# FFN-up GEMM as 2x2x2 block products by Strassen's identity, with weight-block sums made by accumulating DMAs

## The chip, the cores and the metric

One core of one Trainium2 chip. The metric is device microseconds (us) of one execution. Engines are named as in the profile: PE is TensorE (matmuls; PEld its weight loads), DVE is VectorE, ACT is ScalarE, POOL is GpSimd, SP is SyncE, which here only issues DMAs.

## The reference

One step of a streaming encoder with two layers for 640 tokens (512 of a prompt, 8 x 16 of running streams), width 1024, in fp32. Each layer projects x, runs four attention and convolution branches, mixes them, and ends in an FFN. Only the FFN is touched (`d_ff` = 2816):

```python
x = layer_norm(ALPHA * x + mixed, ln1_g, ln1_b)
up = x @ w_up                                   # (640, 1024) @ (1024, 5632)
upc, new_ffn = causal_dwconv(up, past_ffn, ffn_conv_w, ffn_conv_b)   # 3 taps
val, gate = jnp.split(upc, 2, axis=-1)
h = (jax.nn.silu(gate) * val) @ w_down          # (640, 2816) @ (2816, 1024)
x = layer_norm(ALPHA * x + h, ln2_g, ln2_b)
```

## The kernel before

Activations lie transposed, channels on partitions and tokens along the columns. To keep fp32 accuracy every GEMM splits both operands into a high and a low part and does three matmuls for one (`mm3`, L113 to L116). `xh` and `xl` are the parts of x^T, 8 blocks of 128 channels by 640 tokens, in two chunks of tokens, `CH` = 384 + 256, since a PSUM buffer holds 512 columns. `wload` (L103 to L111) fetches 512 KB of weights by a DMA of SP into `wst` (2 buffers), ACT casts the high part `wh` (L108), DVE subtracts to the low part `wl` (L110); `wh` and `wl` are rings of 3. `mtile` (L118) makes 128 output channels from one such weight tile: for each chunk 8 blocks x 3 matmuls into a PSUM buffer `g` (3 buffers).

The FFN's 44 column tiles of w_up make 22 j's: tile j holds values, tile 22 + j gates. `up(j)` (L1093) calls `mtile` for both, copies the results to `ext` on ACT (L1101 to L1103), saves the last columns on POOL (`nf`, L1104, L1105), runs the 3-tap conv (L1108 on ACT, two steps of L1110 on DVE for each tile, into `uac`), then tanh on ACT (`eth`, L1114), three products on DVE (L1115, L1117, L1120), and the split of the result into `hh` (ACT, L1123) and `hl` (DVE, L1124), with 10 buffers each. I call what follows the last matmul of a j its tail.

The down GEMM (`rows_gemm`, L1035) takes the j's in parts, two j's to a pair: parts of 6, 6, 6 and 4 j's. A part runs after the up tiles of its j's, in two halves of 512 output columns; in a half each j gives 5 token tiles x 3 matmuls of 512 columns into PSUM buffers `a` (5) and one `g`, and DVE adds the sums to x (`acx`, L1043, L1045). The last two parts run at the end of the FFN. So PE works through phases of up tiles with down parts between them. The order on each engine is fixed at build time by a scheduler from the program's order and priorities; `wload` has a high priority, so that weights are asked for early.

Of the kernel before, what the change touches and what calls it, by code (L numbers as in the profile page):

```python
# [16 lines left out]
L = 2  # L17
D = 1024
# [16 lines left out]
CH = ((0, 384), (384, 640))  # L35
# [5 lines left out]
def body(tc, I, O):  # L41
# [28 lines left out]

    xh = [perm.tile([128, 8, b - a], F32R, name=f"xh{i}") for i, (a, b) in enumerate(CH)]
    xl = [perm.tile([128, 8, b - a], F32R, name=f"xl{i}") for i, (a, b) in enumerate(CH)]
# [40 lines left out]
    def mm3(ps, ah, al, bh, bl, first, last):  # L113
        pe.matmul(ps, lhsT=ah, rhs=bh, start=first, stop=False)  # L114
        pe.matmul(ps, lhsT=ah, rhs=bl, start=False, stop=False)  # L115
        pe.matmul(ps, lhsT=al, rhs=bh, start=False, stop=last)  # L116

    def mtile(src):  # L118
        wh, wl = wload(src)
        out = []  # L120
        for c, (a, b) in enumerate(CH):
            ps = gps()[:, : b - a]
            for k in range(8):
                mm3(ps, wh[:, k * 128 : k * 128 + 128], wl[:, k * 128 : k * 128 + 128],
                    xh[c][:, k, :], xl[c][:, k, :], k == 0, k == 7)
            out.append(ps)
        return out

    def mtiles(srcs):
        ws = [wload(s) for s in srcs]  # L130
        out = [[] for _ in srcs]
        for c, (a, b) in enumerate(CH):
            for i, (wh, wl) in enumerate(ws):
                ps = gps()[:, : b - a]
                for k in range(8):
                    mm3(ps, wh[:, k * 128 : k * 128 + 128], wl[:, k * 128 : k * 128 + 128],
                        xh[c][:, k, :], xl[c][:, k, :], k == 0, k == 7)
                out[i].append(ps)
        return out

    def xcol(t):
        return (0, t * 128) if t < 3 else (1, (t - 3) * 128)
# [23 lines left out]
    def x_transpose(z, t):  # L166
        c, o = xcol(t)
        for h in range(2):
# [4 lines left out]
            hi = xh[c][:, h * 4 : h * 4 + 4, o : o + 128]  # L173
            act.copy(hi, pv)  # L174
            dve.tensor_sub(xl[c][:, h * 4 : h * 4 + 4, o : o + 128], pv, hi.bitcast(F32))
# [78 lines left out]
def layer(tc, l, I, O, E):  # L254
# [59 lines left out]
    for k in range(2):  # L314
# [107 lines left out]
    for ps, (a, b) in zip(mtile(I["wa"][l, 0]), CH):  # L422
        act.copy(qih[:, a:b], ps)
        dve.tensor_sub(qil[:, a:b], ps, qih[:, a:b].bitcast(F32))
        if b == T:
            act.copy(qs, ps[:, 128:256])
    exts = []
    for k in range(2):
# [156 lines left out]
    for t in range(NT):  # L585
        c, o = xcol(t)
        g1 = gps()[:, :256]
        for k in range(8):
            wh, wl = w1[k // 4]
            ko = (k % 4) * 256  # L590
            mm3(g1, xh[c][:, k, o : o + 128], xl[c][:, k, o : o + 128],
# [422 lines left out]
    df, close_df = op("df", "right")  # L1014
    mh, ml = [], []
    for m in range(8):
# [3 lines left out]
        h_ = mk(df, "hh", T, 10, F32R)  # L1020
        l_ = mk(df, "hl", T, 10, F32R)
# [11 lines left out]
    ep, close_ep = op("ep")  # L1033

    def rows_gemm(parts, hh, hl, src, after):  # L1035
        for pi, kps in enumerate(parts):
# [15 lines left out]
            if not lastp:  # L1052
                for hf in range(2):
                    pst = [aps() if t < 4 else gps() for t in range(NT)]
# [7 lines left out]
            else:  # L1062
                ws = [[wload(src(kp, hf), p=ep, nb=4) for kp in kps] for hf in range(2)]
# [13 lines left out]
    gb = mk(dx, "gb", 2 * D).rearrange("p (i d) -> p i d", i=2)  # L1077
    sp.dma_start(gb, I["ln1"][l].partition_broadcast(128))

    after1 = (lambda t: ln_rows(dx, x[t], t, gb, [], t in (1, 3)), lambda t: x_transpose(x[t], t))  # L1080

    for _ in rows_gemm([[0, 1], [2, 3]], mh, ml, lambda kp, hf: I["wo"][l, hf, kp], after1):
        pass

    sf = mk(ep, "sf", 44 * 16)
# [3 lines left out]
    nfv = nf.rearrange("p (j i) -> p j i", j=44)  # L1089
    hh, hl = {}, {}  # L1090
    first = mtiles([I["wu"][l, jj] for jj in (0, NJ, 1)])

    def up(j):  # L1093
        accs = []
        for i_, jj in enumerate((j, NJ + j)):
# [238 lines left out]
```

## Time and profile before

| | |
|---|---|
| time, median of 3 runs | 2145.78 us (2144.29 to 2147.37) |
| profiled execution: span | 2143.2 us |
| median less this span | 2.6 us |
| PE busy | 2111.0 us, 13284 matmul records |
| DVE, ACT, POOL busy | 1368.2, 767.7, 366.3 us |
| mean granted TensorE clock | 0.997 of full speed |

The span runs from the first to the last instruction of one profiled execution; the durations below come from that execution. Shares are averages over stages with different limits; the FFN of layer 0 lies at about 620 to 1060 us, that of layer 1 at about 1675 to 2143 us.

### The profile page before, as it was taken

To read this page: it belongs to the slowest core of one execution; us is meant where nothing else is said; L and a number is where in the kernel's file an instruction comes from. 1 tells how busy PE (TensorE), PEld (TensorE's weight loads), DVE (VectorE), ACT (ScalarE), POOL (GpSimd) and SP (SyncE) were. 2 spreads that over 40 slices of the span, in tenths; PEclk is the share of its full clock that TensorE was granted. 3 is DMA by queue.
4 is the path that set the end of the run, shared out by engine and by line. 5 is a ranking of instruction groups with operands and counts; after the bars stand their busy time and mean duration, and the time that the engine had idled before them with its cause. 6 is when DMAs were issued, how large, how long until landed. Compare 5 with 4: busy or idle time off the path is not lost.

```text
span 2143.2 us, 33850 instructions
## 1 busy us (share of the span) xinstructions
PE 2111.0 (98%) x13284; PEld 1914.2 (89%) x13284; DVE 1368.2 (64%) x2399; ACT 767.7 (36%) x1520; POOL 366.3 (17%) x595
## 2 busy tenths in 40 slices
PE   6999999999999999999999999999999999999998
PEld 6998979879889898999899898897898998989996
DVE  5899994643476455555679999745246653645656
ACT  4333432322235243344224434223232442424440
POOL 2300001411022021122012000023021220202211
PEclk9999999999999999999999999999999999999999
DMA  8452124442422222222343521354314122222221
GB/s 262 113 167 83 64 87 130 154 135 89 149 75 80 78 70 79 79 70 89 116 113 91 172 80 52 119 156 141 108 62 172 70 71 78 79 70 79 80 85 70
DMA packets 110871, 220.52 MB, mean 103 GB/s; under 512 B 31148, under 2 KB 51408, under 8 KB 110192
## 3 DMA queue, kind: packets, MB, share of 16 engines
q1 hardware_dynamic: 110712, 218.36, 30.8%
q8 instruction: 104, 1.70, 0.3%
q14 instruction: 55, 0.45, 0.1%
HBM read 196.81 MB, written 21.50 MB: 102 GB/s over the span
## 4 chain that ended last, share of the span: by engine, by line
PE 93%; issue 2%; DVE 2%; POOL 2%; ACT 1%; DMA 1%; SPq 0%; POOLq 0%; DVEq 0%; ACTq 0%
PE g L114 22%; PE g L116 22%; PE g L115 21%; PE a L116 6%; PE a L114 6%; PE a L115 6%; PE a L725 1%; PE a L677 1%; PE a L913 1%; PE a L712 1%; PE a L949 1%; PE a L517 1%; PE a L171 1%; PE a L982 1%; PE a L766 0%
## 5 line engine op out<-in xcount | busy, mean ns | idle before, releaser
L114 PE MATMUL g<-xh,wh 128*128 128x256 f32 (+1 forms) x2784 | 867.0, 312 | 2.6 <-ACT xh L174 1.5
L115 PE MATMUL g<-xl,wh 128*128 128x256 f32 (+1 forms) x2784 | 866.0, 311 | 0.1
L116 PE MATMUL g<-xh,wl 128*128 128x256 f32 (+1 forms) x2784 | 863.6, 310 | 0.0
L114 PEld LDWEIGHTS g<-xh,wh 128*128 128x128 f32 x2784 | 524.2, 188 | 17.3 <-issue 9.4
L115 PEld LDWEIGHTS g<-xl,wh 128*128 128x128 f32 x2784 | 525.6, 189 | 6.7 <-issue 5.0
L116 PEld LDWEIGHTS g<-xh,wl 128*128 128x128 f32 x2784 | 525.1, 189 | 6.7 <-issue 5.8
L110 DVE TENSOR_TENSOR wl<-wst,wh 128x1024 fp32r<-128x1024 f32 (+1 forms) x248 | 302.0, 1219 | 338.1 <-ACT wh L108 337.8
L108 ACT CAST wh<-wst 128x1024 fp32r<-128x1024 f32 (+1 forms) x248 | 258.3, 1043 | 527.3 <-PE g L115 269.6
L116 PE MATMUL a<-wh,hl 128*128 128x512 f32 x512 | 202.6, 397 | 0.0
L115 PE MATMUL a<-wl,hh 128*128 128x512 f32 x512 | 201.5, 394 | 0.0
L114 PE MATMUL a<-wh,hh 128*128 128x512 f32 x512 | 200.9, 395 | 0.0
L1104 POOL COPY nf<-ext 128x2 f32<-128x2 f32 x88 | 93.4, 1061 | 478.6 <-ACT ext L1102 478.6
L1110 DVE SCALAR_TENSOR_TENSOR uac<-ext,pc,uac 128x656 f32<-128x656 f32 x176 | 158.3, 900 | 9.6 <-ACT uac L1108 0.4
L851 POOL TENSOR_TENSOR acx<-acx,gt 128x640 f32<-128x640 f32 x32 | 52.7, 1648 | 387.1 <-DVE gt L842 241.4
L115 PEld LDWEIGHTS a<-wl,hh 128*128 128x128 f32 x512 | 96.1, 188 | 23.5
L116 PEld LDWEIGHTS a<-wh,hl 128*128 128x128 f32 x512 | 96.1, 188 | 22.9
L114 PEld LDWEIGHTS a<-wh,hh 128*128 128x128 f32 x512 | 96.0, 188 | 22.2
L842 DVE SCALAR_TENSOR_TENSOR gt<-gt,g 128x384 f32<-128x384 f32 (+1 forms) x96 | 45.8, 483 | 106.0 <-PE g L116 106.0
L1101 ACT COPY ext<-g 128x384 f32<-128x384 f32 x88 | 42.2, 480 | 155.1 <-PE g L116 91.9
L826 ACT ACTIVATE gt<-g 128x384 f32<-128x384 f32 (+1 forms) x128 | 55.4, 433 | 112.9 <-PE g L116 109.2
L619 DVE SCALAR_TENSOR_TENSOR cacc<-cep,pc,cacc 128x512 f32<-128x512 f32 x120 | 89.6, 747 | 0.1
L1108 ACT ACTIVATE uac<-ext,pc 128x656 f32<-128x656 f32 x88 | 82.8, 941 | 4.7 <-ACT ext L1103 0.4
(316 smaller groups left out, 2831.6 us busy)
## 6 DMA issues: line engine op xcount, KB each, us to landing
wst<-in_wu SPq DMA_DIRECT2D x88, 512.0 KB, 3.5
wst<-in_wg SPq DMA_DIRECT2D x64, 512.0 KB, 3.8
wst<-in_wd SPq DMA_DIRECT2D x44, 512.0 KB, 3.6
wst<-in_wa SPq DMA_DIRECT2D x22, 512.0 KB, 3.5
wbs<-in_wb SPq DMA_DIRECT2D x64, 128.0 KB, 2.2
cd<-in_c_bv SPq DMA_DIRECT2D x32, 256.0 KB, 3.9
ca<-in_c_bkT SPq DMA_DIRECT2D x32, 256.0 KB, 2.7
wst<-in_wo SPq DMA_DIRECT2D x16, 512.0 KB, 3.5
```

The source lines that it names most:

```text
L108: act.copy(wh[:, :cols], st[:, :cols])
L110: dve.tensor_sub(wl[:, :cols], st[:, :cols], wh[:, :cols].bitcast(F32))
L114: pe.matmul(ps, lhsT=ah, rhs=bh, start=first, stop=False)
L115: pe.matmul(ps, lhsT=ah, rhs=bl, start=False, stop=False)
L116: pe.matmul(ps, lhsT=al, rhs=bh, start=False, stop=last)
L619: dve.scalar_tensor_tensor(a_[:, 0:TP], ep_[:, j : j + TP], w, a_[:, 0:TP], op0=ALU.mult, op1=ALU.add)
L826: act.activation(g_[:, a:b], ps, AF.Tanh, scale=0.5)
L842: dve.scalar_tensor_tensor(dst[:, a:b], g_[:, a:b], 1.0, ps, op0=ALU.add, op1=ALU.mult)
L851: pool.tensor_tensor(acc[m], acc[m], g_, op=ALU.add)
L1104: pool.tensor_copy(nfv[:, jj, 0:2], ext[:, 512:514])
L1108: act.activation(ac, ext[:, 2:658], AF.Identity, scale=wc[2], bias=pc[:, PC_FB + jj : PC_FB + jj + 1])
L1110: dve.scalar_tensor_tensor(ac, ext[:, i : i + 656], wc[i], ac, op0=ALU.mult, op1=ALU.add)
```

## The change

Chunks become 320 + 320 tokens (`HT` = 320), and `xh` and `xl` one tile each. For j = 0 and 1 the up tiles are made as before. For j = 2 to 21 the value and the gate tile are taken together: w_up's block for j is [k-half 0, k-half 1] x [gates, values], x^T is [k-half 0, k-half 1] x [tokens 0 to 319, 320 to 639], and the 2 x 2 result comes from seven products instead of eight (`seven`), each of 4 blocks x 3 matmuls of 320 columns. The sums of x blocks, T1 to T4, are made once a layer on DVE from a raw copy of x^T (`raw`, written by ACT at the transposes) and split to parts (`split_t`). The sums of weight blocks are made for each j in a staging tile `sg` of 7 blocks (2 buffers): SP's DMAs fill it with 1.79 MB, and three DMAs issued by POOL add to it in place; four casts and four subtractions turn it into `wh` and `wl`, in the same ring of 3 as the down weights.

Three PSUM buffers collect the products: A takes a11, s2, s3, a22 one after the other, C takes s1 and s4, B takes a12; between them ACT copies A to `sn` tiles, and DVE and ACT form the four blocks in `ext` from these. The conv and the rest of `up` are unchanged. `ext` has 3 buffers instead of 2, `hh` and `hl` 6 instead of 10; the down parts are 2, 4, 4, 4, 4 and 4 j's, the first four of them each after its own j's, the last two at the end, so that the up phases have 2 + 4, 4, 4 and 8 j's. Down parts use `a` alone.

```diff
-CH = ((0, 384), (384, 640))
+HT = 320
+CH = ((0, HT), (HT, 640))
...
-    def x_transpose(z, t):
+    def x_transpose(z, t, raw=None):
...
+            if raw is not None:
+                act.copy(raw[h][:, :, tc_], pv)
...
+    r11, r12, r21, r22 = raw[0][:, :, lo_], raw[0][:, :, hi_], raw[1][:, :, lo_], raw[1][:, :, hi_]
+    dve.tensor_sub(r22, r22, r12)
+    dve.tensor_sub(r12, r11, r12)
+    dve.scalar_tensor_tensor(r11, r22, -1.0, r11, op0=ALU.mult, op1=ALU.subtract)
+    dve.scalar_tensor_tensor(r21, r11, -1.0, r21, op0=ALU.mult, op1=ALU.subtract)
+    xo = {"b11": (xh[:, k0, lo_], xl[:, k0, lo_]), "b21": (xh[:, k1, lo_], xl[:, k1, lo_]),
+          "b22": (xh[:, k1, hi_], xl[:, k1, hi_]), "t4": (xh[:, k0, hi_], xl[:, k0, hi_])}
...
-    def up(j):
+    def stage(j):
+        with tc.high_priority(offset=4000):
+            sg = mk(up_, "sg", 7 * 512, 2)
+            v = sg.rearrange("p (b c) -> p b c", b=7)
+            w = I["ws"][l, j].rearrange("p (b c) -> p b c", b=4)
+            sp.dma_start(v[:, 1:6:4], w[:, 0:2])
+            sp.dma_start(v[:, 4], w[:, 0])
+            sp.dma_start(v[:, 0:4:3], w[:, 2:4])
+            sp.dma_start(v[:, 2:7:4], w[:, 2:4])
+            pool.dma_start(v[:, 1:5:3], w[:, 1:3], accum_op=ALU.add)
+            pool.dma_start(v[:, 2:7:4], v[:, 1:2].to_broadcast([128, 2, 512]), accum_op=ALU.add)
+            pool.dma_start(v[:, 6], w[:, 2], accum_op=ALU.add)
+            out = []
+            for i in range(4):
+                n = 1024 if i < 3 else 512
+                src = sg[:, i * 1024 : i * 1024 + n]
+                wh = mk(perm, "wh", 1024, 3, F32R)
+                act.copy(wh[:, :n], src)
+                wl = mk(perm, "wl", 1024, 3, F32R)
+                dve.tensor_sub(wl[:, :n], src, wh[:, :n].bitcast(F32))
+                out += [(wh[:, q : q + 512], wl[:, q : q + 512]) for q in range(0, n, 512)]
+        return out
...
+    def product(ps, w, xop, first):
+        wh, wl = w
+        bh_, bl_ = xo[xop]
+        for k in range(4):
+            o = slice(k * 128, k * 128 + 128)
+            mm3(ps, wh[:, o], wl[:, o], bh_[:, k], bl_[:, k], first and k == 0, k == 3, more=not first)
...
+    def seven(j):
+        a11, s1, s2, a12, s3_, a22, s4 = stage(j)
+        ev, sv = ext_tile(j)
+        eg, sg_ = ext_tile(NJ + j)
+        A, C = gps()[:, :HT], gps()[:, :HT]
+        product(A, a11, "b11", True)
+        p1 = mk(up_, "sn", HT, 3)
+        act.copy(p1, A)
+        product(C, s1, "t1", True)
+        product(A, s2, "t2", False)
+        u2 = mk(up_, "sn", HT, 3)
+        act.copy(u2, A)
+        B = gps()[:, :HT]
+        product(B, a12, "b21", True)
+        dve.tensor_tensor(ev[:, 2 : 2 + HT], p1, B, op=ALU.add)
+        product(A, s3_, "t3", False)
+        u3 = mk(up_, "sn", HT, 3)
+        act.copy(u3, A)
+        n = TP - HT
+        dve.scalar_tensor_tensor(eg[:, 2 + HT : 514], C[:, :n], -1.0, u3[:, :n], op0=ALU.mult, op1=ALU.subtract)
+        dve.scalar_tensor_tensor(sg_[:, :, 2:18], s3(C[:, n:]), -1.0, s3(u3[:, n:]), op0=ALU.mult, op1=ALU.subtract)
+        product(A, a22, "t4", False)
+        act.mul(eg[:, 2 : 2 + HT], A, -1.0)
+        product(C, s4, "b22", False)
+        dve.tensor_tensor(ev[:, 2 + HT : 514], u2[:, :n], C[:, :n], op=ALU.add)
+        dve.tensor_tensor(sv[:, :, 2:18], s3(u2[:, n:]), s3(C[:, n:]), op=ALU.add)
+        return (ev, sv), (eg, sg_)
...
+    halves = [I["ws"][l, j][:, c : c + 1024] for j in range(2) for c in (1024, 0)]
+    pus = mtiles(halves[:3]) + [mtile(halves[3])]
+    for nm, src in (("t1", r12), ("t2", r11), ("t3", r22), ("t4", r21)):
+        split_t(nm, src)
...
-    parts = [[0, 1, 2], [3, 4, 5], [6, 7, 8], [9, 10]]
+    parts = [[0], [1, 2], [3, 4], [5, 6], [7, 8], [9, 10]]
...
         for kp in kps:
-            up(2 * kp)
-            up(2 * kp + 1)
-        if i < 2:
+            for j in (2 * kp, 2 * kp + 1):
+                if j >= 2:
+                    up(j, seven(j))
+        if i < len(parts) - 2:
             next(run)
```

PE's order before, where layer 0's first up phase ends and its down part begins (`g` is the last up tile, hh_6949 belongs to j0, hh_7038 to j1, hh_7473 to j4 and hh_7618 to j5):

```order
L116 MATMUL g_7576<-xh_64,wl_7549 128x256
L114 MATMUL a_7622<-wh_7629,hh_6949 128x512
L115 MATMUL a_7622<-wl_7631,hh_6949 128x512
...
L116 MATMUL g_7626<-wh_7629,hl_6950 128x512
L114 MATMUL a_7622<-wh_7629,hh_7038 128x512
...
L116 MATMUL g_7626<-wh_7701,hl_7474 128x512
L114 MATMUL a_7622<-wh_7701,hh_7618 128x512
```

The same place in the changed kernel, the end of the phase of j2 to j5 (g_7656 is C with the product s4 of j5; hh_7471 belongs to j3, hh_7621 to j4, hh_7771 to j5):

```order
L117 MATMUL g_7656<-xh,wl_7647 128x320
L116 MATMUL a_7777<-wl_7784,hh_7471 128x512
...
L117 MATMUL a_7779<-wh_7782,hl_7472 128x512
L115 MATMUL a_7775<-wh_7818,hh_7621 128x512
...
L117 MATMUL a_7779<-wh_7818,hl_7622 128x512
L115 MATMUL a_7775<-wh_7818,hh_7771 128x512
```

Between the last up matmul and the first row that reads the newest hh there stood 75 matmuls (5 j's x 15); now there are 8 rows of j3 and 15 of j4, the rest of the down half's rows on j2 and j3 having moved ahead of the last products. The phases that end with j9 and j13, and those of layer 1, read alike.

DVE's order in the changed kernel from the end of that last product on (ext_7649 and uac_7756 are the values of j5, uac_7762 the gates; wl_7866 and wl_7902 are down weights):

```order
L1185 TENSOR_TENSOR ext_7649<-sn_7695,g_7656 128x192 [waits PE_49]
L1186 TENSOR_TENSOR ext_7649<-sn_7695,g_7656 128x8x16
L111 TENSOR_TENSOR wl_7866<-wst_7862,wh_7864 128x1024 [waits DMAHW5_49,Activation_49]
L1198 SCALAR_TENSOR_TENSOR uac_7756<-ext_7649,pc_341,uac_7756 128x656 [waits Activation_49]
L1198 SCALAR_TENSOR_TENSOR uac_7762<-ext_7652,pc_341,uac_7762 128x656 [waits Activation_49]
L1198 SCALAR_TENSOR_TENSOR uac_7756<-ext_7649,pc_341,uac_7756 128x656 [waits DVE_49]
L111 TENSOR_TENSOR wl_7902<-wst_7898,wh_7900 128x1024 [waits DMAHW6_49,Activation_49]
L1198 SCALAR_TENSOR_TENSOR uac_7762<-ext_7652,pc_341,uac_7762 128x656 [waits DVE_49]
L1203 SCALAR_TENSOR_TENSOR uac_7762<-eth_7766,uac_7762 128x656 [waits Activation_49]
L1205 SCALAR_TENSOR_TENSOR eth_7766<-uac_7762,uac_7756 128x512 [waits DVE_49]
L1208 SCALAR_TENSOR_TENSOR eth_7766<-uac_7762,uac_7756 128x128
L1212 TENSOR_TENSOR hl_7772<-eth_7766,hh_7771 128x640 [waits Activation_49]
```

The evacuation of s4 and two subtractions of weights now stand between the last product and the newest hh, and the values' conv, which used to be done while the gate tile's matmuls ran, comes after the last product.

POOL's order in the changed kernel for one j within a phase (sg_8239 is its staging tile; the copies to nf belong to the j whose staging tile it takes over):

```order
L1126 DMA sg_8239<-in_ws 128x2x512 [waits DMAHW2_49,DMAHW1_49,DMAHW7_49,DMASW6_49,DVE_49]
L1192 COPY nf_6767<-ext_7966 128x2 [waits DVE_49]
L1193 COPY nf_6767<-ext_7966 128x16 [waits DVE_49]
L1127 DMA sg_8239<-sg_8239 128x2x512 [waits DMAHW4_49,DMASW2_49]
L1192 COPY nf_6767<-ext_7963 128x2 [waits DVE_49]
L1193 COPY nf_6767<-ext_7963 128x16 [waits DVE_49]
L1128 DMA sg_8239<-in_ws 128x512 [waits DMASW3_49]
```

Before, POOL's queue held only the memsets and the copies; now three DMAs of each j stand in it, the second waiting for the first and the third for the second, and the next j's first comes behind them.

## Rows read from the trace of the kernel before

**Rows 1.** The page, part 1: busy time, share of the span, instructions.

```profile
PE 2111.0 (98%) x13284; PEld 1914.2 (89%) x13284; DVE 1368.2 (64%) x2399; ACT 767.7 (36%) x1520; POOL 366.3 (17%) x595
```

**Rows 2.** Windows: busy us by engine, granted clock, DMA share, GB/s.

```profile
620.00:1010.00 390.00, 390.00 (x2467) 373.54 (x2466) 213.31 (x252) 159.57 (x272) 77.83 (x172) 1.00 0.22 78
...
0.00:30.00 30.00, 12.91 (x47) 11.21 (x48) 21.01 (x22) 16.59 (x26) 12.93 (x23) 1.00 0.86 292
```

**Rows 3.** Timeline of PE: start, duration, what, in up tiles and a down part.

```profile
689.83 0.34 PE L116 MATMUL g<-xh,wl 128*128 128x384 f32 x1
...
692.95 0.34 PE L116 MATMUL g<-xh,wl 128*128 128x384 f32 x1
693.13 0.28 PE L114 MATMUL g<-xh,wh 128*128 128x256 f32 x1
...
695.84 0.28 PE L116 MATMUL g<-xh,wl 128*128 128x256 f32 x1
...
702.94 0.40 PE L114 MATMUL a<-wh,hh 128*128 128x512 f32 x1
...
720.45 0.39 PE L114 MATMUL a<-wh,hh 128*128 128x512 f32 x1
```

**Rows 4.** Timeline of ACT: the last hh of that phase.

```profile
711.10 0.72 ACT L1123 CAST hh<-eth 128x640 fp32r<-128x640 f32 x1
```

**Rows 5.** DVE's groups by line and form, 620 to 1010 us.

```profile
L1110 DVE SCALAR_TENSOR_TENSOR uac<-ext,pc,uac 128x656 f32<-128x656 f32 x86 | 77.3, 900 | 4.8 <-ACT uac L1108 0.4
L110 DVE TENSOR_TENSOR wl<-wst,wh 128x1024 fp32r<-128x1024 f32 x55 | 67.4, 1225 | 132.5 <-ACT wh L108 132.4
L1115 DVE SCALAR_TENSOR_TENSOR uac<-eth,uac 128x656 f32<-128x656 f32 x21 | 17.7, 842 | 23.4 <-ACT eth L1114 23.4
L1124 DVE TENSOR_TENSOR hl<-eth,hh 128x640 fp32r<-128x640 f32 x21 | 17.2, 819 | 0.8 <-ACT hh L1123 0.8
...
L1120 DVE SCALAR_TENSOR_TENSOR eth<-uac,uac 128x128 f32<-128x128 f32 x21 | 6.0, 285 | 0.0
...
L1045 DVE TENSOR_TENSOR acx<-acx,a 128x512 f32<-128x512 f32 x8 | 5.5, 690 | 3.9 <-PE a L116 3.8
```

**Rows 6.** ACT's groups by line and form, 620 to 1010 us.

```profile
L108 ACT CAST wh<-wst 128x1024 fp32r<-128x1024 f32 x55 | 57.7, 1049 | 141.3 <-PE g L115 78.5 <-PE g L116 50.5 <-DVE acx L1043 5.9
L1108 ACT ACTIVATE uac<-ext,pc 128x656 f32<-128x656 f32 x43 | 40.5, 941 | 2.4 <-ACT ext L1103 0.4
L1101 ACT COPY ext<-g 128x384 f32<-128x384 f32 x44 | 21.1, 480 | 77.5 <-PE g L116 46.8 <-DVE uac L1110 30.5
L1114 ACT ACTIVATE eth<-uac 128x656 f32<-128x656 f32 x21 | 15.8, 754 | 6.3 <-DVE uac L1110 6.3
```

**Rows 7.** Windows, and PE's timeline around a stop in layer 1.

```profile
617.00:620.00 3.00, 2.76 (x20) 2.73 (x20) 3.00 (x7) 1.75 (x4) 0.00 (x0) 1.00 0.00 0
...
1142.00:1145.00 3.00, 3.00 (x15) 2.96 (x16) 2.82 (x7) 1.33 (x4) 2.86 (x8) 0.50 0.58 165
...
1141.83 0.47 PE L375 MATMUL a<-ident,cqn 128*128 128x128 f32 x1 [1.95 <-ACT cqn L367]
...
1142.17 0.56 PE L114 MATMUL g<-xh,wh 128*128 128x256 f32 x1
...
1145.29 0.28 PE L116 MATMUL g<-xh,wl 128*128 128x256 f32 x1
```

**Rows 8.** DMA issues of 620 to 1010 us: KB each, us to landing.

```profile
wst<-in_wu SPq DMA_DIRECT2D x39, 512.0 KB, 3.5
...
gb<-in_ln SPq DMA_DIRECT2D x1, 1024.0 KB, 4.6
```

**Rows 9.** POOL's groups by line and form, 620 to 1010 us.

```profile
L1104 POOL COPY nf<-ext 128x2 f32<-128x2 f32 x43 | 45.6, 1061 | 234.0 <-ACT ext L1102 234.0
...
L1099 POOL MEMSET ext<- 128x2 f32 x42 | 4.2, 99 | 74.0 <-DVE uac L1110 44.4 <-ACT ext L1101 29.5
```

**Rows 10.** Weight loads by line and form, 620 to 1010 us.

```profile
L114 PEld LDWEIGHTS g<-xh,wh 128*128 128x128 f32 x698 | 130.9, 188 | 0.1
```

More of the change, by code (lines that the diff above doesn't have):

```diff
@@ L111, in wload, with mm3 @@
         return wh, wl
[L113 to L116, printed above, removed]
+    def mm3(ps, ah, al, bh, bl, first, last, more=False):
+        pe.matmul(ps, lhsT=ah, rhs=bh, start=first, stop=False, skip_group_check=more)
+        pe.matmul(ps, lhsT=ah, rhs=bl, start=False, stop=False, skip_group_check=more)
+        pe.matmul(ps, lhsT=al, rhs=bh, start=False, stop=last, skip_group_check=more)
     def mtile(src):
@@ L1032, in layer, with rows_gemm @@
         sp.dma_start(x[t], xd[l][t])
-    ep, close_ep = op("ep")
-    def rows_gemm(parts, hh, hl, src, after):
+    def rows_gemm(parts, hh, hl, src, after, wp):
         for pi, kps in enumerate(parts):
@@ L1053, in rows_gemm @@
                 for hf in range(2):
-                    pst = [aps() if t < 4 else gps() for t in range(NT)]
+                    pst = [aps() for t in range(NT)]
                     for kp in kps:
@@ L1062, in rows_gemm @@
             else:
-                ws = [[wload(src(kp, hf), p=ep, nb=4) for kp in kps] for hf in range(2)]
+                p = wp()
+                ws = [[wload(src(kp, hf), p=p, nb=4) for kp in kps] for hf in range(2)]
                 for t in range(NT + 2):
@@ L1089, in layer @@
     nfv = nf.rearrange("p (j i) -> p j i", j=44)
-    hh, hl = {}, {}
-    first = mtiles([I["wu"][l, jj] for jj in (0, NJ, 1)])
-    def up(j):
-        accs = []
-        for i_, jj in enumerate((j, NJ + j)):
-            pu = first[2 * j + i_] if 2 * j + i_ < 3 else mtile(I["wu"][l, jj])
-            ext = mk(ep, "ext", 658, 2)
-            sev = ext[:, 514:658].rearrange("p (s i) -> p s i", s=NS)
-            pool.memset(ext[:, 0:2], 0.0)
-            pool.tensor_copy(sev[:, :, 0:2], sfv[:, jj])
-            act.copy(ext[:, 2:386], pu[0])
-            act.copy(ext[:, 386:514], pu[1][:, 0:128])
-            act.copy(sev[:, :, 2:18], s3(pu[1][:, 128:256]))
+    up_, close_up = op("up")
@@ new lines, in layer, with split_t @@
+    for nm in ("t1", "t2", "t3"):
+        xo[nm] = tuple(mk(up_, f"{nm}{q}", 4 * HT, 1, F32R).rearrange("p (k n) -> p k n", k=4) for q in "hl")
+    def split_t(nm, src):
+        h_, l_ = xo[nm]
+        act.copy(h_, src)
+        dve.tensor_sub(l_, src, h_.bitcast(F32))
+    hh, hl = {}, {}
+    def stage(j):
[20 more added lines that the diff above has]
+        return out
@@ new lines, in regular @@
+    def regular(jj, pu):
+        ext, sev = ext_tile(jj)
+        act.copy(ext[:, 2 : 2 + HT], pu[0])
+        act.copy(ext[:, 2 + HT : 514], pu[1][:, 0 : TP - HT])
+        act.copy(sev[:, :, 2:18], s3(pu[1][:, TP - HT :]))
+        return ext, sev
+    def seven(j):
[25 more added lines that the diff above has]
+        return (ev, sv), (eg, sg_)
@@ L1104, in up @@
+    def up(j, pair):
+        accs = []
+        for jj, (ext, sev) in zip((j, NJ + j), pair):
             pool.tensor_copy(nfv[:, jj, 0:2], ext[:, 512:514])
             pool.tensor_copy(s3(nfv[:, jj, 2:18]), sev[:, :, 16:18])
-            ac = mk(ep, "uac", 656, 2)
+            ac = mk(up_, "uac", 656, 2)
             wc = [pc[:, PC_FW + jj * 3 + i : PC_FW + jj * 3 + i + 1] for i in range(3)]
```

94 lines of the change are left out of this document (57 added, 37 removed).

## The prediction, made before the changed kernel had run

> **What bounds the kernel now.** I began with the busy times of the page: PE is busy for 2111.0 of 2143.2 us, DVE for 64% and ACT for 36% [rows 1]. Then I took the window of the stage that is changed: from 620 to 1010 us, most of layer 0's FFN, PE is busy in every microsecond at the full clock, with DVE at 213.31 of 390 us and the DMA engines at 0.22 of their share [rows 2]. So this stage lasts as long as its matmuls, and fewer columns shorten it until another engine or a transfer takes over. The price of a column is in PE's timeline, as distances between starts [rows 3]: 18 matmuls of 384 columns lie between 689.83 and 692.95 (0.1733 us each), 23 of 256 between 693.13 and 695.84 (0.1178), 75 of 512 between 702.94 and 720.45 (0.2335). That is a straight line: 320 columns cost 0.1455 us.
>
> **What it removes.** A j took 2 tiles x 8 blocks x 3 matmuls, each as 384 + 256 columns: 48 x (0.1733 + 0.1178) = 13.97 us. The other chunks, 320 + 320, cost the same 0.291 us a pair, so the chunk size alone is worth nothing. Seven products of 4 x 3 matmuls of 320 columns are 84 x 0.1455 = 12.22 us. The saving is 1.746 us for a j; 20 j's in each of 2 layers give **-69.8 us**. Everything else has a price.
>
> **The ends of the four-j phases.** Before, the down part that follows an up phase covers six j's: PE has 75 matmuls for j0 to j4 (17.5 us, [rows 3]) before it touches the newest hh, as the order's rows show. The newest j's tail then lay in the open and cost nothing: the down part starts at 702.94 [rows 3], ACT writes the newest hh from 711.10 to 711.82 [rows 4], and PE never waited. After, three phases in each layer have four j's, and only 8 + 15 rows stand between the last product and the first row on j5's hh: 23 x 0.2335 = 5.4 us. The tail does not get shorter. From the end of the last product: two evacuations 0.35 + 0.29 (0.69 at 512 columns and 0.285 at 128 give the line, [rows 5]); ACT's uac 0.94 [rows 6], to 1.9 us with the hand-over; then DVE's row as ordered, a wl 1.22 beside it, conv steps of 0.90 with another wl 1.23 between them, to 7.1; eth 0.75, to 7.95; 0.84 + 0.69 + 0.29, to 9.75; hh 0.72 [rows 4], to 10.5 us. PE waits 10.5 - 5.4 = about 5 us, six times: **+30 us**. Bounds: 2 us each if the two wl and the hand-overs drop out (12), 7 us if DVE arrives 2 us late (42).
>
> **The clock after a stop.** At 1141.83 PE had stood still for 1.95 us, and from 1142 to 1145 the granted clock was 0.50, 1.2 GHz: 14 matmuls of 256 columns took from 1142.17 to 1145.29, 3.12 us instead of 14 x 0.1178 = 1.65 [rows 7]. With the transposes around them I count 1.8 us lost. A short gap in 617 to 620 left the clock at 1.00 [rows 7]. Six stops of 5 us resemble the first: 6 x 1.8 = **+11 us** (0 to 15).
>
> **The entry into the products.** Once a layer, the casts and splits of T1 to T4 stand on ACT and DVE between the four regular tiles and the first j by products, and t4 overwrites a part of xh that the regular tiles still read. The first wh waits behind an xh cast that waits for PE; then come the cast (1.05) and wl (1.22) [rows 5, 6], which nothing covers: about 2.5 us, twice, **+5 us** (2 to 12).
>
> **DVE and ACT within a phase.** For one j DVE has 3 wl and a half one (3 x 1.225 + 0.69, as 512 columns take elsewhere), 4 conv steps (3.60), 0.84 + 0.82 + 0.69 + 0.29, and five evacuations of 320, 192 and 128 columns, by the line 1.76: together 12.36 us against PE's 12.22 [rows 5]. Before, it had about 8.7 against 13.97. ACT has 8.8: casts 3.7, four copies of 320 columns by 0.42, uac, eth, hh [rows 6]. The excess on DVE is 0.14 us for a j, 5.6 us over 40, and the down parts and a lag of up to about 2.7 us absorb most of it. But DVE works in order, and one wl of each j waits for a cast that can start only when a product ends: up to 0.6 us for a j, 24 in all. Below: 0. I take **+9 us**.
>
> **The accumulating DMAs.** This kernel has no DMA issued by POOL, so their price is not in its trace. In POOL's queue each j has first accumulation, second (which waits for the first), third (which waits for the second), then the next j's; so a j needs S = the first two, 512 KB each, one after the other. How much S is hidden: there are two sg buffers. The first j's buffer is free about 4.8 us into its phase and filled some 4.5 us later (3.5 for one load of 512 KB, [rows 8]; 1.79 MB at the 340 GB/s of the first 30 us, 292 at a share of 0.86, would be 5.3, [rows 2]). So the k-th j of a phase has its sums at 9.3 + (k - 2) S and needs them at 12.22 (k - 1) + 1.2, which is its third product less a cast and a wl. For four j's that stalls PE by 2S - 28.6, for the eight at the end by 6S - 77.4, where positive. S up to 12.9 us is free. Bounds: 2 x 3.5 = 7 from the plain loads; each sum reads two operands for one result, so the row of twice the size, 1024 KB in 4.6 us [rows 8], gives 9.2; the loads alone need 1.79 MB in 12.22 us, 0.43 of 340 GB/s, and 9.2 / 0.57 = 16 if the sums get only the rest. I take 11, near the 1024 KB row with a microsecond for each issue: **0**, with both ends kept.
>
> The POOL queue itself speaks against that value: its copy of 2 columns takes 1.06 us on average where a memset of 2 columns takes 0.10 [rows 9], in a stage where DVE is half idle; after, DVE hardly rests. The Trainium skill has a rule for it ("SBUF — State Buffer", section "SBUF: two separate sides"): POOL and some DVE operations share a port as an exclusive lock, and descriptors of a DMA issued from POOL can't be written while DVE holds it. The slow copy agrees that POOL waits, but no row shows a DMA doing so; by this rule each issue would wait out a DVE instruction, and the sum would go to the first rival's. The Trainium skill's own fit for such a DMA ("DMA: Bandwidth & Descriptors", section "Anatomy of one DMA — SWDGE (gpsimd) path"), 2.0 us + bytes at 436 GB/s, makes an estimate of 3.2 us for 512 KB, and the sum would stay as it is.
>
> The rest is small. Two more down parts in a layer add 20 evacuations of 0.69 us [rows 5] on DVE, beside down matmuls; the copies of raw x go to ACT, which has time.
>
> **Sum.** -69.8 + 30 + 11 + 5 + 9 = -14.8 us. Against the profiled execution: 2143.2 - 14.8 = 2128.4 of span, and 2.6 us outside it as before (the median 2145.78 less the span): **2131 us**.
>
> **Rivals.** (1) *The accumulations are late*: slower. Place: the eight-j phase, then the others. It decides at 2 x (6S - 77.4) = 14.8, S = 14.1 us. With S = 16: 18.6 + 3 x 3.4 in a layer, 57.6 in all, 2189 us; S = 18 gives about 2236. For it: a serial queue, POOL's waits, a bound of 16. Against: DMA share 0.22 now. (2) *The tails are covered better*: if DVE runs ahead, or the wl between the conv steps do not wait for casts, six stops of 2 us without loss of clock cost 12 instead of 41: 2102; with none at all 2090. For it: a whole down half of transfers is ready at these points. Against: the ordered DVE row, with each step waiting for ACT. (3) *DVE is the bound*: a j takes 12.9 us instead of 12.22, 27 us over 40 in place of 9, and each tail begins 2 us late (+12): 2161. For it: 12.36 of 12.22. Against: the down phases, where it can catch up. (4) *The change does not do what it says*: 84 matmuls are no cheaper than 96 because something other than columns sets their pace, such as the weight load of 188 ns [rows 10]. Rows of 256 columns at 0.118 us with the same loads speak against it; 2201 us.
>
> **How the numbers follow.** My forecast, 2117 to 2146, gets 0.43; the better tails 0.16; late accumulations 0.27; DVE as the bound 0.11; no saving 0.03. A difference under 0.2% (4.3 us) can't be told from none. Faster than 2141.5: four fifths of the first and all of the second, and a little of the third, 0.54; within 4.3 us 0.11; slower 0.35. The better tails reach to 2090 and late accumulations past 2189; leaving out a tenth at each end makes the range 2098 to 2189.
>
> **What would show it.** Right: matmuls of 320 columns start 0.1455 us apart; in each layer three stops of PE of about 5 us, before the down rows of j5, j9 and j13, with a granted clock near 0.5 behind them; no wait of ACT's cast (L1134) for a DMA; DVE near 100% in the last up phase. Wrong: PE's stops are spread over every j, with the cast waiting for sg's DMAs (first rival), or the stops are absent (second), or PE waits for wl or a PSUM buffer in each j (third).

## The result, and the profile after

The changed kernel took 2307.03 us (median of 4 runs, 2302.52 to 2308.21) against 2146.57 us: a ratio of 1.0744 (1.0729 to 1.0759), 160 us slower. The forecast was 2131 us, faster, in a range of 2098 to 2189; the first rival, late accumulations, is what happened. The page of the changed kernel, part 1, the answer to [rows 1], and the software queue's line of part 3 (packets, MB, share of the DMA engines):

```profile
span 2305.7 us, 33790 instructions
PE 2123.0 (92%) x12804; PEld 1896.5 (82%) x12804; DVE 1517.2 (66%) x2735; ACT 843.6 (37%) x1548; POOL 483.3 (21%) x715
...
q0 software_dynamic: 27520, 52.44, 13.7%
```

PE has 480 matmuls less in the records, and yet its busy time rose by 12.0 us and its idle time (span less busy) from 32.2 to 182.7 us. Together that is the 162.5 us by which the span grew. What PE waited for, by the view of waits (engine, tile and line, releaser: us, times, longest):

```profile
PE g L115 <- ACT ext L1183: 58.2, 14, 6.1
PE a L115 <- ACT hh L1211: 40.0, 6, 8.2
PE g L115 <- ACT wh L1134: 22.9, 21, 3.6
...
PE a L115 <- DVE acx L1043: 7.7, 2, 3.9
PE g L115 <- ACT sn L1178: 7.3, 22, 0.4
```

The six stops at hh are the forecast tails, 40 us for 30. The largest item, 14 stops of up to 6.1 us, was not in my list by that name: PE is about to begin a j's product s1 (its operand is t1h) and waits for ACT to evacuate a PSUM buffer, the A of the j before (L1183). The timelines of SP, POOL, ACT and PE in the last phase of layer 0 show why ACT is late:

```profile
1019.27 0.37 SPq L1122 DMA_DIRECT2D sg<-in_ws  x1
...
1011.99 0.91 POOL L1128 DMA_DIRECT2D sg<-in_ws  x1 [9.41 <-DMA sg<-sg]
...
1014.73 1.32 POOL L1126 DMA_DIRECT2D sg<-in_ws  x1
...
1021.98 1.21 POOL L1127 DMA_DIRECT2D sg<-sg  x1 [4.91 <-DMA sg<-in_ws]
1031.74 0.90 POOL L1128 DMA_DIRECT2D sg<-in_ws  x1 [8.55 <-DMA sg<-sg]
...
1080.10 1.21 POOL L1127 DMA_DIRECT2D sg<-sg  x1 [3.64 <-DVE ext L1175]
...
1085.94 0.90 POOL L1128 DMA_DIRECT2D sg<-in_ws  x1 [3.73 <-DMA sg<-sg]
...
1031.55 1.04 ACT L1134 CAST wh<-sg 128x1024 fp32r<-128x1024 f32 x1 [7.85 <-DMA sg<-sg]
1032.50 0.43 ACT L1183 ACTIVATE ext<-g 128x320 f32<-128x320 f32 x1
...
1028.70 0.31 PE L117 MATMUL g<-xh,wl 128*128 128x320 f32 x1
1032.98 0.64 PE L115 MATMUL g<-t1h,wh 128*128 128x320 f32 x1 [3.98 <-ACT ext L1183]
```

POOL's queue makes one j in 19.75 us, from one third accumulation (L1128) to the next: 2.74 us until the first is issued, 7.25 until it has landed and the second is issued, 9.76 until that has landed. ACT's next cast needs the second sum and stands idle for 7.85 us, and the evacuation of A, which needs no DMA at all, stands behind it in ACT's queue. PE waits for that. So from the fourth on the j's of this phase, the last with eight j's in layer 0, come 19.3 to 20.0 us apart instead of 12.2, and PE is stopped once in each.

The second accumulation does not always take 9.76 us. SP issues the next j's 1.79 MB in four DMAs from 1019.27 to 1021.14 (the first is shown), and POOL issues the second accumulation right behind it, at 1021.98. At 1080.10, at the end of the phase, SP has nothing more to load, and the same accumulation lets POOL go on after 5.84 us. Worked out from the records of the whole trace: 15 of the 40 second accumulations had less than 0.2 MB of SP's transfers beside them and landed in 5.0 to 6.1 us; the other 25 had 0.6 to 2.6 MB beside them and landed in 7.1 to 12.5 us.

The windows answer to those of [rows 2] and [rows 7]: three j's of that phase, and 9 us of it.

```profile
1013.00:1072.40 59.40, 45.89 (x252) 43.88 (x253) 33.47 (x52) 24.06 (x37) 21.61 (x40) 0.87 0.71 160
...
1033.00:1036.00 3.00, 3.00 (x11) 3.00 (x12) 3.00 (x5) 2.74 (x5) 3.00 (x7) 0.50 0.57 87
1036.00:1039.00 3.00, 3.00 (x13) 3.00 (x12) 3.00 (x5) 1.35 (x3) 1.05 (x3) 0.50 0.65 106
1039.00:1042.00 3.00, 3.00 (x21) 3.00 (x21) 1.53 (x3) 1.23 (x2) 0.94 (x3) 0.97 0.92 197
```

After a stop of 3.98 us the clock was granted at 0.50, its level of 1.2 GHz, for about 6 us. DVE, my third rival, is busy for 33.5 of 59.4 us. The answer to [rows 8] for POOL's DMAs, part 6 of the page:

```profile
sg<-in_ws POOLq DMA_DIRECT2D x40, 512.0 KB, 7.0
sg<-sg POOLq DMA_DIRECT2D x40, 512.0 KB, 9.2
...
sg<-in_ws POOLq DMA_DIRECT2D x40, 256.0 KB, 4.4
```

By stages, from PE's timelines: the two FFNs take 141 us more than before (74 and 67), the branch mix's GEMM with its layer norm 13.5 us more in both layers together, the attention part of layer 1 about 6 us more.

### The profile page after: what moved, and what is told of

It reads as the page before. It is cut to its first block, busy times and chain, and to the rows that moved or that the text cites. A ratio compares the mean times of both kernels' runs of the same rounds, so it can differ in the third digit from the quotient of the medians.

```text
span 2305.7 us, 33790 instructions
## 1 busy us (share of the span) xinstructions
PE 2123.0 (92%) x12804; PEld 1896.5 (82%) x12804; DVE 1517.2 (66%) x2735; ACT 843.6 (37%) x1548; POOL 483.3 (21%) x715
## 3 DMA queue, kind: packets, MB, share of 16 engines
q0 software_dynamic: 27520, 52.44, 13.7%
## 5 line engine op out<-in xcount | busy, mean ns | idle before, releaser
L115 PE MATMUL g<-xh,wh 128*128 128x320 f32 x2144 | 675.9, 316 | 28.0 <-ACT wh L1134 18.3
L116 PE MATMUL g<-xl,wh 128*128 128x320 f32 x2144 | 667.7, 312 | 0.9 <-DVE xl L173 0.8
L117 PE MATMUL g<-xh,wl 128*128 128x320 f32 x2144 | 663.9, 312 | 0.8 <-DVE wl L1136 0.8
L115 PEld LDWEIGHTS g<-xh,wh 128*128 128x128 f32 x2144 | 403.8, 189 | 51.0 <-ACT wh L1134 23.8
L116 PEld LDWEIGHTS g<-xl,wh 128*128 128x128 f32 x2144 | 404.5, 189 | 9.6 <-issue 5.6
L117 PEld LDWEIGHTS g<-xh,wl 128*128 128x128 f32 x2144 | 403.5, 189 | 8.6 <-issue 7.0
L1136 DVE TENSOR_TENSOR wl<-sg,wh 128x1024 fp32r<-128x1024 f32 (+1 forms) x160 | 174.1, 1089 | 211.0 <-ACT wh L1134 209.2
L109 ACT CAST wh<-wst 128x1024 fp32r<-128x1024 f32 (+1 forms) x168 | 174.2, 1038 | 312.0 <-PE g L116 168.7
L1134 ACT CAST wh<-sg 128x1024 fp32r<-128x1024 f32 (+1 forms) x160 | 150.4, 940 | 358.7 <-DMA sg<-sg 128.1
L111 DVE TENSOR_TENSOR wl<-wst,wh 128x1024 fp32r<-128x1024 f32 (+1 forms) x168 | 204.8, 1220 | 74.3 <-ACT wh L109 68.3
L116 PEld LDWEIGHTS a<-wl,hh 128*128 128x128 f32 x600 | 118.1, 197 | 32.2 <-DVE wl L111 5.1
```

The source lines that it names most:

```text
L109: act.copy(wh[:, :cols], st[:, :cols])
L111: dve.tensor_sub(wl[:, :cols], st[:, :cols], wh[:, :cols].bitcast(F32))
L115: pe.matmul(ps, lhsT=ah, rhs=bh, start=first, stop=False, skip_group_check=more)
L116: pe.matmul(ps, lhsT=ah, rhs=bl, start=False, stop=False, skip_group_check=more)
L117: pe.matmul(ps, lhsT=al, rhs=bh, start=False, stop=last, skip_group_check=more)
L1134: act.copy(wh[:, :n], src)
```

## Experiments

Times of one run stand without a range, beside one run of the kernel before at 2144 to 2145 us; the others are medians of several rounds, with ratio and interval.

**1. Without the sums.**

```diff
-            pool.dma_start(v[:, 1:5:3], w[:, 1:3], accum_op=ALU.add)
-            pool.dma_start(v[:, 2:7:4], v[:, 1:2].to_broadcast([128, 2, 512]), accum_op=ALU.add)
-            pool.dma_start(v[:, 6], w[:, 2], accum_op=ALU.add)
```

> The changed kernel without its three accumulating DMAs: the sums of weight blocks are left out, so v1, v2, v4 and v6 of the staging tile hold single blocks; loads, casts, products and all else stay. Theory A (the sums arrive late: a j needs them about 20 us apart where its products take 12.2): the stops before t1's products go away, a j of the last phase takes 12.2 to 13 us instead of 19.8, and only the stops at the ends of the four-j phases (40 us in all) with their clock loss remain: 2140 to 2160 us. Theory C (DVE at its limit and the tails make the products unprofitable by themselves, the sums only fill that time): 2220 us or more, and a j still takes 15 us or more.

2186.26 us. The stops before t1's products are gone; a window of three j's of the last phase:

```profile
988.30:1026.70 38.40, 37.71 (x254) 36.95 (x254) 33.44 (x51) 24.43 (x36) 6.76 (x24) 1.00 0.32 99
```

That is 12.8 us for a j. So leaving out the sums gains 121 us. But 2186 lies above the 2140 to 2160 that I expected, and 42 us above the time before, without any accumulating DMA: other steps of the prediction failed too. The stops at hh are 29.6 us here.

**2. Plain DMAs of POOL in place of the adding ones** (the edit takes `accum_op` out of the three).

> The three DMAs of POOL's queue stay, with the same shapes, sources and order, but copy instead of add: the sums are left out. Theory A1 (reading the destination and adding makes them slow): 512 KB land in about 4 us instead of 7.0 and 9.2, the two in a row take about 9 us, under the 12.9 that are free, and the time is that of the kernel without the sums, within 15 us. Theory A2 (the path through POOL is slow, its issue and its small descriptors): the two still take 14 us or more, and the time stays above 2250 us.

2182.65 us, as without any. The three DMAs in this run, with the same shapes, bytes and queue, and the software queue's line:

```profile
sg<-in_ws POOLq DMA_DIRECT2D x40, 512.0 KB, 4.9
sg<-sg POOLq DMA_DIRECT2D x40, 512.0 KB, 3.4
...
sg<-in_ws POOLq DMA_DIRECT2D x40, 256.0 KB, 5.7
...
q0 software_dynamic: 14720, 52.44, 7.2%
```

The first two together take 8.3 us, under the 12.9 that are free. So three DMAs of each j in POOL's queue, each waiting for the one before, are not late by themselves. But the edit changes more than the adding. The same 52.44 MB now go in 14720 packets, where the adding DMAs made 27520 of them. And the j's come faster, so that SP's loads now meet the third DMA (5.7 us here, 4.4 with adding) and no longer the second: the medians 9.2 and 3.4 were not taken under like conditions. With next to nothing of SP's beside it the transfer within SBUF takes 5.0 to 5.5 us when it adds and about 3.1 when it copies. How much of this is the adding and how much the packets is not shown.

**3. The second accumulation without its wait for the first.**

```diff
-            pool.dma_start(v[:, 2:7:4], v[:, 1:2].to_broadcast([128, 2, 512]), accum_op=ALU.add)
+            pool.dma_start(v[:, 2:7:4], w[:, 1:2].to_broadcast([128, 2, 512]), accum_op=ALU.add)
```

> The second accumulating DMA takes its 512 KB from the weights in HBM instead of from the sums that the first has just made, so it need not wait for the first (v2 and v6 lack one addend); bytes, number and adding stay, apart from the source. Theory B1 (the chain is the price: two latencies in a row): both are in flight together, a j of the last phase takes 12.2 to 14 us, the time is 2150 to 2190 us. Theory B2 (the DMA engines' rate is the price): each of the two takes longer when they overlap, about 14 us, a j of the last phase stays above 17 us, and the time above 2260 us.

2222.02 us: between the two expectations. 512 KB take 7.5 us each (median) when two are in flight, and a j of the last phase 12.8 to 14.4 us in layer 0, up to 16.5 in layer 1. So 85 of the 121 us go away when the second accumulation need not follow the first. They are not the price of the chain alone, since the edit also moves the source to HBM and the second accumulation's place among SP's loads. Of the 36 us that are left, 12 are at the stops for hh (42.1 us here, 29.6 without sums); the rest is not divided.

**4. Down parts behind by one pair.**

```diff
-    parts = [[0], [1, 2], [3, 4], [5, 6], [7, 8], [9, 10]]
+    parts = [[0, 1], [2, 3], [4, 5], [6, 7], [8, 9], [10]]
+    ups = [[0, 1, 2], [3, 4], [5, 6], [7, 8], [9, 10], []]
...
-    for i, kps in enumerate(parts):
+    for i, kps in enumerate(ups):
```

> The changed kernel in full, with the down parts behind by one pair of j's: parts of 4, 4, 4, 4, 4 and 2 j's, each run two j's later than its own last j, so that every phase by products has four j's and no part needs the newest hh. Theory of the tail (the six stops of 5 to 8 us are the newest j's way through DVE and ACT): these stops and their clock loss go away, about 58 us, and the eight-j phase with its 40 us of late sums becomes two of four j's with about 10 each, 20 a layer: about 2210 us, 2190 to 2235. If the stops are in truth a wait for late sums or for DVE, they only move, and the time stays above 2270 us.

2217.16 us, in the range: no stop at hh is left, and eight of the ten phases of four j's, all but the last of each layer, have one stop for late sums. One of them, and the row of the second accumulation:

```profile
968.44 0.64 PE L115 MATMUL g<-t1h,wh 128*128 128x320 f32 x1 [5.57 <-ACT ext L1183]
...
sg<-sg POOLq DMA_DIRECT2D x40, 512.0 KB, 5.7
```

The tails are a price of their own, and with the eight-j phase gone the sums are hidden for three j's of four. The second accumulation lands in 5.7 us by the median here, and in 9.2 in the changed kernel: 23 of 40 now have little of SP's loads beside them (5.0 to 6.0 us), the other 17 still take up to 13.5 us.

**5. The sums on POOL itself.**

```diff
+            sx = mk(up_, "sx", 512, 2)
+            sp.dma_start(v[:, 5], w[:, 1])
+            sp.dma_start(sx, w[:, 0])
+            sp.dma_start(v[:, 0:4:3], w[:, 2:4])
+            pool.tensor_tensor(v[:, 1], sx, v[:, 5], op=ALU.add)
+            pool.tensor_tensor(v[:, 2], v[:, 1], v[:, 0], op=ALU.add)
+            pool.tensor_tensor(v[:, 4], sx, v[:, 0], op=ALU.add)
+            pool.tensor_tensor(v[:, 6], v[:, 2], v[:, 3], op=ALU.add)
```

> The changed kernel in full, with the sums of weight blocks made by four additions of 512 columns on POOL from 1 MB of plain loads, instead of 1.79 MB of loads and three accumulating DMAs. POOL adds 640 columns in 1.64 us in another stage, so four of 512 are about 5.3 us for a j, under 12.2. Theory A (only the late sums make the difference between the changed kernel and the one without sums): as without sums, 2186 us, within 15. Rival (POOL's additions take a port that DVE needs, and DVE is the next bound): a j of the last phase takes over 13.5 us and the time is 2215 us or more.

2238.54 us: both signs of the rival came, with 13.4 to 16.3 us for a j of the last phase, 15.0 on average. DVE's groups by line and form, here (951 to 1060 us) and in the kernel without sums (936 to 1030 us), and between them a wait of PE that the kernel without sums does not have:

```profile
L1137 DVE TENSOR_TENSOR wl<-sg,wh 128x1024 fp32r<-128x1024 f32 x22 | 31.8, 1448 | 8.3 <-ACT wh L1135 8.3
L1213 DVE TENSOR_TENSOR hl<-eth,hh 128x640 fp32r<-128x640 f32 x6 | 9.3, 1550 | 0.0
L1176 DVE TENSOR_TENSOR ext<-sn,g 128x320 f32<-128x320 f32 x8 | 3.8, 478 | 2.3 <-PE g L117 2.3
```

```profile
PE g L115 <- DVE ext L1176: 20.6, 15, 1.8
```

```profile
L1133 DVE TENSOR_TENSOR wl<-sg,wh 128x1024 fp32r<-128x1024 f32 x22 | 26.9, 1223 | 12.1 <-ACT wh L1131 11.7 <-DMA sg<-in_ws 0.3
L1209 DVE TENSOR_TENSOR hl<-eth,hh 128x640 fp32r<-128x640 f32 x6 | 4.9, 819 | 0.0
L1172 DVE TENSOR_TENSOR ext<-sn,g 128x320 f32<-128x320 f32 x7 | 3.4, 481 | 2.3 <-PE g L117 2.3
```

Beside POOL's additions the two operations of DVE that read two inputs from SBUF take 0.2 and 0.7 us longer on average; the one with an input in PSUM (g) does not. The Trainium skill ("SBUF — State Buffer", section "SBUF: two separate sides") names a port that POOL and DVE share: a DVE operation with two SBUF inputs and a POOL operation that reads SBUF exclude each other there for a whole instruction. These rows agree with it for DVE's operations. That DVE thereby sets the pace of the phase is not shown: in experiment 13 it has as much work and the kernel is faster.

**6. Sums on POOL and down parts behind**, both edits.

> The sums on POOL and the down parts behind by one pair, both edits together, in full. If the tails' six stops (30 us without accumulating DMAs) and the clock lost behind them (about 2.3 us each) are a price of their own, this is 45 us under the kernel with the sums on POOL alone: about 2141 us, 2128 to 2156, about the time before the change. If DVE is the bound, the stops turn into waits within the phases and the gain is under 20 us.

2176.71 us: 62 under the fifth experiment, more than the 45 expected, but from a higher start, so that the time itself lies above its range.

**7. What was taken outside the products, put back.**

```diff
-CH = ((0, HT), (HT, 640))
+HC = 384
+CH = ((0, HC), (HC, 640))
...
-                    pst = [aps() for t in range(NT)]
+                    pst = [aps() if t < na else gps() for t in range(NT)]
```

(`na` is 4 in the branch mix's GEMM, 5 in the FFN's.)

> The changed kernel in full, with two things put back outside the products: chunks of 384 + 256 tokens for all other GEMMs, and a g buffer for the fifth token tile in the GEMM of the branch mix (w_out), which the change had taken from it. The trace shows 13 us more than before in that GEMM with its layer norm, and 6 us more in the rest of layer 1's attention part. If these two edits are their cause: about 2288 us, 2280 to 2298. If the raw copies of x or the code around them are the cause, the time stays above 2300.

2294.23 us, ratio 1.0699 (1.0681 to 1.0717): 13 us less by the medians. In PE's timelines of the profiled executions the branch mix's GEMM again takes 40.1 us in each layer (45.5 and 46.5 in the changed kernel), and the attention part of layer 1 is about 6 us shorter. With five `a` buffers for five token tiles the second half of that GEMM waits for DVE to add the first (`acx L1043` above, 3.9 us at most).

**8. All three edits**: sums on POOL, down parts behind, outside put back.

> All three edits together: sums on POOL, down parts behind by a pair, chunks and the fifth buffer put back outside the products. If the three prices add: 2141 - 19 = 2122 us, 2108 to 2140, faster than before the change by about 1%. If one of them only moves a wait, 2150 or more.

2168.3 us, ratio 1.0104 (1.0089 to 1.0119), above its range. POOL's additions keep their price: a phase of four j's with its down part takes about 83.4 us, as long as the same work before (4 x 13.97 + 28 = 83.9).

**9. The same without sums.**

> The changed kernel without its sums (as in the first experiment: single blocks in place of the sums), with the down parts behind by a pair and the two things put back outside the products: what is left when sums, tails and the stages outside cost nothing. Without sums 2186; less the six stops and the clock behind them, 45; less 13 for what was put back: 2128 us, 2115 to 2142, under the time before. If the phases by products are slow for another reason (a j takes 12.8 us there and not 12.2, and each phase's first j 13.7), it stays at 2140 or more, and no way of making the sums could pay by more than 0.3%.

2125.41 us, ratio 0.991 (0.9894 to 0.9927), as expected. A phase takes 79.4 us. This is what the products gain here if the sums cost nothing: 20 us, not 70. Ten phases at 79.4 instead of 83.9 us would be 45 us; where the other 25 go is not shown.

**10. The sums ahead of time**, by accumulating DMAs from HBM to HBM while the gates of the same layer run.

```diff
+        if s < NJ:
+            sp.dma_start(sd[s][:, 0:4:2, 0:1], g_[:, 0:2].unsqueeze(2))
+            sp.dma_start(sd[s][:, 0:2], ws(s)[:, 0:1].to_broadcast([128, 2, 512]))
+            sp.dma_start(sd[s][:, 2:4], ws(s)[:, 2:4])
+        if 2 <= s - 1 < NJ:
+            pool.dma_start(sd[s - 1][:, 0:2], ws(s - 1)[:, 1:3], accum_op=ALU.add)
...
+            sp.dma_start(v[:, 1:5:3], sd[j][:, 0:2])
```

> In full: the sums are made by accumulating DMAs from HBM to HBM, into scratch tensors, while the branch gates of the same layer run (each j's copies are tied to one gate tile, so they spread over that part), and the FFN loads the seven blocks by plain DMAs of SP; the down parts behind by a pair, and the two things put back outside the products. If the price of the accumulating DMAs is only their place next to the products: the time of the kernel without sums and tails, 2128 us, plus up to 15 where POOL's queue waits for sums and the gates' additions stand behind: 2128 to 2145, under the time before or equal. If 45 MB more a layer slow the weight loads of that part or POOL blocks the gates: 2160 or more.

2395.65 us, ratio 1.1158 (1.1135 to 1.1182). Both fears came true: POOL's queue stood still for sums (first line) and ACT for the gate that POOL had not yet added (second), and a gate's weights took 8.1 us to land instead of 3.8.

```profile
POOL sd L283 <- DMA sd<-in_ws: 256.7, 35, 14.4
...
ACT gt L845 <- POOL acx L871: 84.3, 9, 23.1
...
wst<-in_wg SPq DMA_DIRECT2D x64, 512.0 KB, 8.1
```

**11 and 12. Mixed**: accumulating DMAs for three j's of four, and for the fourth (`j % 4 == 1`) the four additions of the fifth experiment, on POOL or on DVE; down parts behind, outside put back.

> In full: down parts behind by a pair, the two things put back outside the products, and of each four j's the first three get their sums by accumulating DMAs as in the change, the fourth by four additions on POOL. With all by accumulating DMAs this would be 2217 - 13 = 2204 us, of which the fourth j's stop before t1's product (about 5 us and 3 us of clock behind it, ten times) is the largest part that is left. If the two chains in a row that the fourth j waits for are the cause: about 75 us less, and about 15 us back for DVE beside POOL's additions in a quarter of the j's: 2144 us, 2128 to 2162, within 0.8% of the time before. If the third j is late as well once the fourth is not, the stops move there and the time is 2175 or more.

> The same with the fourth j's four additions on DVE. At 0.69 us each they are 2.8 us of DVE work in ten of 40 j's, and DVE has nothing to spare within a phase: 2129 without them and up to 28 us more: 2150 us, 2135 to 2168. If they are cheaper than POOL's, since the port is not shared: under the kernel with POOL's additions by 3 us or more.

On POOL 2164.16 us, ratio 1.0089 (1.007 to 1.0108), above its range. On DVE 2133.96 us, ratio 0.9937 (0.9919 to 0.9955): faster than the kernel before, by 0.6%, and the best complete version found here.

**13. All sums on DVE** (the additions of the fifth experiment as `dve.tensor_tensor`, for every j).

> In full: down parts behind by a pair, the two things put back outside the products, and the sums of every j by four additions on DVE, from 1 MB of plain loads; no accumulating DMA is left. The prediction held DVE to be at its limit within a phase (12.36 us of work for 12.22). If so, 2.8 us more make a j at least 15 us, of which the down parts (28 us for four j's, with 14 us of DVE work) take up a part: at least 2125 + 40 x 1.5 = 2185 us. If PE's own waits for ACT's copies set the 12.8 us of a j, and half of the sums can be made while a down part runs: 2135 to 2160.

2145.37 us, ratio 0.9994 (0.9984 to 1.0005). From the third phase of a layer on, a phase takes 79.6 us, as without sums (79.4), with 2.8 us more of DVE work in each j; of the 20 us about 9 are lost in each layer's first two phases (170 us to the third, 161 without sums). So it was not DVE's load that set the 79.4 us. The second half of such a phase, with most of its down part, DVE busy for 40.9 of 43.3 us:

```profile
928.30:971.60 43.30, 43.07 (x245) 38.98 (x244) 40.93 (x64) 21.72 (x29) 17.64 (x22) 1.00 0.34 103
```

**14. The copy of A to u3 moved ahead of s3**, without sums.

```diff
-        product(A, s3_, "t3", False)
         u3 = mk(up_, "sn", HT, 3)
         act.copy(u3, A)
+        product(A, s3_, "t3", False)
```

> The kernel without sums, with the down parts behind by a pair and the two things put back, and in addition ACT's copy of A to u3 is made before the product s3 instead of behind it (so u3 holds the wrong partial result; sums and this value are left out of the computation, the work of every engine is the same). If PE's wait for that copy is what makes a j 12.8 us instead of 12.3: 12.3 to 12.4 us a j and 2125 - 40 x 0.45 = 2107 us, 2100 to 2114. If DVE's load makes it: no change, 2121 to 2129.

2157.84 us, ratio 1.0052 (1.0035 to 1.0068): neither. The waits for the copy are gone, but the scheduler made another order, with two rows of the next j's a11 ahead of s3, and PE now waits there for the cast of their weights, about 1 us each time, in a j of 13.9 us. The edit did not isolate the copy. It does show that with the same operations on every engine the order alone moves a j by 1.1 us.

## Why the prediction was wrong, by its own steps

**The accumulating DMAs** are the step that failed: they were mis-sized, and that decided the sign. I took S = 11 us, from plain loads that had their time to themselves, and stalls of nothing. Measured in the last phase are 7.25 + 9.76 = 17.0 us, and the queue has another 2.74 us between two j's that I had left out: 19.75, against 12.9 that are free. About 4 of the 9.76 us go with SP's loads of the next j, which are issued just ahead of the second accumulation; with nothing beside it the same DMA takes 5.0 to 5.5 us, and the first two together about 12, near the 11 that I took. My working had this in its bound of 16, where the sums get only the rate that the loads leave; I set it aside with the DMA share of 0.22, which was the average of a kernel that loads less for each j (1.05 MB against 1.79 by SP alone). The bound was still too low by the 2.74 us in the queue. The rest of the step came out roughly: with S = 19.75 its formulas give 2 x (41 + 3 x 11) = 148 us; leaving the sums out gained 121 (experiment 1).

My working also had the wrong carrier: it let PE wait for its weights, but most of the wait reached PE over an evacuation behind a cast in ACT's queue. No run moves that evacuation alone. POOL's queue makes one j in 19.75 us whatever carries the wait, so the order on ACT would not bring the j's of the eight-j phase closer together.

The Trainium skill's fit for a DMA of POOL's ("DMA: Bandwidth & Descriptors", section "Anatomy of one DMA — SWDGE (gpsimd) path"), by my estimate 3.2 us, is near the copy within SBUF (3.4 us), below the one from HBM (4.9), and far from the additions (7.0 and 9.2). The Trainium skill's rule of the port ("SBUF — State Buffer", section "SBUF: two separate sides") is not seen to set this price: the copies of experiment 2 go through the same queue with DVE busy for 33.4 of 38.4 us, and they are not late.

**The ends of the four-j phases** were right in place, number and size: six stops, 29.6 us without the sums (30 forecast), and the first tail there takes 10.4 us (10.5 forecast) from the last product to the end of hh; experiment 4 removed them. With the sums the stops are 40.0 us; why they are longer is not shown.

**The clock after a stop** was priced for six stops, and it is lost after the stops for sums too. With 40 x (13.97 - 84 x 0.1466) = 66 us of columns less, PE is busy for 12 us more, so about 78 us of its busy time are slow matmuls and other gaps. That sum is an estimate; no experiment gives the clock alone.

**What it removes**: 320 columns start 0.1466 us apart (24 of them between 1039.39 and 1042.91 us; 0.1455 forecast), -66 us instead of -69.8.

**DVE and ACT within a phase** was 9 us for DVE at its limit. Without sums a j takes 12.8 us, 0.58 more than forecast, 23 us over 40. DVE's load is not the cause (experiment 13). PE's waits there are for ACT (wh and sn, 10.1 and 5.1 us in experiment 1); which row of the order to change stays open after experiment 14.

**The entry** (5 us) was not tried by itself; the stop there is 2.0 us in each layer in experiment 9.

**What I called small** was not: I wrote down that the down parts use `a` alone and did not look where else the same function is called. It cost 12 us at the branch mix. The chunk size, which I had priced at nothing from the columns, goes by the place with the 6 us in the attention part, which has no such GEMM; experiment 7 put both back together and does not part them.

**Sum.** Without the sums I would have forecast 2131 us; 2186 was measured. Of the 55 us between, the stages outside the FFN are about 18 (12 + 6), the waits within phases 14 (23 for 9), the columns 4; the other 19, the clock behind the stops among them, I can't assign.

## What to carry to other kernels

Where an operation's price is not in the trace and the sign hangs on it, measure that operation before the whole, and beside the transfers that will run with it: the second accumulation took 5.0 us with nothing beside it and up to 12.5 behind the next j's loads. Count the time between two uses of a queue as well as the transfers in it (2.74 of 19.75 us). Look at which evacuations follow a cast that waits for a transfer: here 58 us of PE's waits came that way. A saving of 12.5% of the up matmuls (66 to 70 us) was worth at most 20 us here, since waits within the phases and stages outside them took back part of it, and part is not assigned; taking a consumer one step behind its producer (experiment 4) gave back 90 us, the sums on POOL alone (experiment 5) 69.

## What the runs showed of the hardware

How long an accumulating DMA takes depends on what it meets. In the changed kernel 512 KB within SBUF landed in 5.0 to 6.1 us with less than 0.2 MB of SP's transfers beside it, and in 7.1 to 12.5 us with 0.6 to 2.6 MB; the medians of 9.2 us there and 5.7 in experiment 4 are mixtures of the two. From HBM it is 7.0 us by the median in one and 6.9 in the other. Adding DMAs made 27520 packets of the same 52.44 MB that plain ones moved in 14720.

DVE's additions cost less than POOL's in the same place: 2134 against 2164 us for a quarter of the j's, 2145 against 2168 for all. Beside POOL's additions DVE's operations on two SBUF operands took up to 0.7 us longer each, but DVE is busy for about the same time in both kernels with all sums (1601 us with its own additions, 1593 beside POOL's), so this alone does not account for the difference, and what does is not shown.
